# Compressed scores spread between the rows of two gate chunks, and three smaller moves around them

## The chip, the cores and the metric

The program runs on one core of a Trainium2 chip. A core has a matrix engine (TensorE, PE in the profile, with its weight loads as PEld), a vector engine (VectorE, DVE), a scalar engine (ScalarE, ACT), GpSimd (POOL), and queues that start DMA transfers (SP's queue here). Each engine works through its own list of instructions in the order in which the list was written; a semaphore holds an instruction back until what it needs is there. The metric is the time on the device of one execution, in microseconds, as the median of several runs.

## The reference

One layer of a decoder trunk on 256 tokens of 1024 channels, in float32:

```
h = rms_norm(x, norm_mix_g)
u_conv, q, kc, vc, ks, vs, kw, vw, g_heads, g_conv, g_attn = split(h @ w_in)
conv = silu(layer_norm(depthwise_31_taps(a * sigmoid(gate)))) @ conv_pw_w
o = g0 * attend(q, compressed kc, vc) + g1 * attend(q, ks, vs) + g2 * attend(q, kw, vw)
x = x + (sigmoid(g_conv) * conv + sigmoid(g_attn) * o) @ w_out
x = x + cross_attention(rms_norm(x, norm_x_g), mem, xq_w, xkv_w, xo_w)
x = x + swiglu(rms_norm(x, norm_ffn_g), ffn_in_w, ffn_out_w)
return rms_norm(x, final_norm_g)
```

There are 16 heads of 64 channels in 4 groups. With 256 tokens all four blocks of 64 keys are selected, so the selected and the window branch are two causal attentions over the same 256 positions with keys and values of their own; the compressed branch attends to 15 compressed blocks. `g0`, `g1`, `g2` are sigmoids of 48 logits per token (three for each head).

## The kernel before

**Products.** Each weight matrix is cut into chunks of 256 output channels, and each chunk comes by DMA in two halves of 128 x 1024 floats. A half is split into a high part (ScalarE copies it to fp32r, L173) and a low part (VectorE subtracts, L174; both in `split`). A chunk's product is six *rows* of eight matmuls with 256 columns each (`rows`, L238): for each half high times high, high times low, low times high. PE needs the high part for the first row of a half and the low part for its third. Raw halves have three buffers, high and low parts four each, so a transfer or a split starts when an earlier half has been used.

**Order.** The order of each engine's list is settled when the program is built, by a scheduler that goes by priorities; `in_line()` and `behind(...)` add orderings by hand (the first keeps a matmul behind the last row on PE, the second keeps what stands in it behind given instructions). The code order around the change is: convolution input (`u`), compressed keys and values (`kc`, `vc`), queries (`q0` to `q3`), then `ks`, `kw`, `vs`, `vw`, the 48 gate logits (`wg`, `g_ps`, L217 to L219, whose sigmoid `sgn` is L594 on ScalarE), the attention gates `ga0` to `ga3` (`gate(j)`), and the attention over eight pairs of heads, between whose parts the rows of `gc0` to `gc3` and `v0` to `v3` are dealt out by `rest(n)`.

**The convolution's taps** run beside all this. VectorE accumulates taps in PSUM (`taps_v`, L404, tiles `yp`), ScalarE multiplies taps (`taps_g`, L418, tiles `vw`, four buffers) for GpSimd to add (L420, `yt`); a few products are GpSimd's own (L416). `convolve(n_v, n_g, *marks)` issues the next `n_v` of VectorE's instructions and `n_g` of the other chain, behind its marks. `part67`, the last result of VectorE's taps, is added by GpSimd at L424. Note that `vw` in the profile is two things: the tap products (L416, L418, L420) and the weight chunk `vw` with its parts `vw_0h`, `vw_0l`, `vw_1h`, `vw_1l` (L173, L174, L238).

**Compressed scores.** After `ga0`, 32 matmuls of 32 columns (L650, `cs_ps`) give the scores of 16 heads in two halves of the queries. VectorE adds them to the bias (`nsc`, L653), takes the minimum, subtracts it (L655, L656) and spreads the compressed values over heads (L661, `vals`). Two transposes bring the sigmoids of the 48 gate logits to the layout of the queries (`gt_ps`, L669, after `ga1`), and VectorE takes the reciprocals (L670, L671).

**Attention.** For each pair of heads `scores` issues eight matmuls (L690, tile `s`, and L692, tile `s0`); VectorE adds the bias and takes the minimum (L695, L700), ScalarE exponentiates (L709, L713), VectorE normalizes (L716 to L723). One pass of the loop issues the scores of the next pair, some rows, the transposes of this pair's weights (`turned`: two of tile `pt_a`, then after one row `pt_b`, L734), whose copies ScalarE makes (`ptt_a`, `ptt_b`, L737), some rows more, and the weighted sums (`output`, tile `o`, L744 to L752). In the first pass the compressed weights are transposed too (`pc_ps`, L821; copy `pct`, L823).

**PSUM.** Tiles with one tag share buffers: "s0" has one (in turn `g_ps`, one half of the compressed scores, the gate transposes `gt_ps`, then the scores `s0` and `pt_b` of each pair), "o" has one, "s" and "pt" two each. A new tile waits until the last reader of the old one is done.

Of the kernel before, what the change touches and what calls it, by code (L numbers as in the profile page):

```python
# [15 lines left out]
P = 128  # L16
# [80 lines left out]
def tile_hybrid_block(  # L97
# [46 lines left out]
    def aux(name, shape, tag, bufs):  # L144
        return axp.tile(shape, F32, tag=tag, name=name, bufs=bufs)

    def f(ap):
        return ap.bitcast(F32)
# [20 lines left out]
    def split(w, shape, name):  # L169
        hi = small(f"{name}h", shape, F32R, tag="whi", bufs=4)  # L170
        lo = small(f"{name}l", shape, F32R, tag="wlo", bufs=4)
        with behind(*first.get(name, ())):
            nc.scalar.activation(hi, w, AF.Copy)  # L173
            nc.vector.tensor_tensor(out=lo, in0=w, in1=f(hi[:]), op=ALU.subtract)  # L174
        return hi, lo


    first = {}

    def behind(*marks):  # L180

# [42 lines left out]
    def in_line():  # L224
        return behind(*last)
# [321 lines left out]
    for j in range(4):  # L547
        ps = whole(f"q{j}", hf)
        q0, q1 = ([qt[j // 2][:, 4 * (j % 2) + 2 * b + k] for b in range(2)] for k in range(2))
        for b in range(2):  # L550
            nc.scalar.activation(q0[b][0:64], ps[0:64, b], AF.Copy, scale=-0.125)
            act = nc.scalar.activation(q1[b][64:128], ps[64:128, b], AF.Copy, scale=-0.125)
        for b in range(2):
            nc.vector.scalar_tensor_tensor(out=q0[b][64:128], in0=ps[0:64, b], scalar=-0.125, in1=f(q0[b][0:64]),
                                           op0=ALU.mult, op1=ALU.subtract)
            vec = nc.vector.scalar_tensor_tensor(out=q1[b][0:64], in0=ps[64:128, b], scalar=-0.125, in1=f(q1[b][64:128]),
                                                 op0=ALU.mult, op1=ALU.subtract)
        convolve((12, 11, 8, 3)[j], 5, act, vec)
        with behind(*last):
            if j == 0:  # L560
                hidden()
            elif j == 2:
                compressed()
# [16 lines left out]
    for br, name in enumerate(("vs", "vw")):  # L580
        ps = gemm_nat(name, h)
        act = nc.scalar.activation(vst[:, :, br], ps, AF.Copy)
        convolve(3, 3 + TAPS * br, act)
    ng = 3 * HEADS
    wg = small("wg", [P, NB, ng], tag="w", bufs=3)
    nc.sync.dma_start(wg, wgn)
# [43 lines left out]
            js = slice(j, j + 2)  # L630
            nc.vector.tensor_tensor(out=yt[:, js], in0=yt[:, js], in1=rl.unsqueeze(1).to_broadcast([P, 2, S]), op=ALU.mult)

    def gate(j):
        return nc.scalar.activation(sga[:, 2 * j:2 * j + 2], gemm(f"ga{j}", h), AF.Sigmoid)

    gate(0)


    sums = small("sums", [P, HEADS, 2, 2])
# [3 lines left out]
    def qh(hd, qb):  # L643
        return qt[hd // 8][:, hd % 8, qb * P:qb * P + P]

    for qb in range(2):
        cs_ps = aux(f"cs_ps{qb}", [P, HEADS, 2, 16], *(("s0", 1), ("s", 2))[qb])
        for hd in range(HEADS):
            with in_line():
                mm = nc.tensor.matmul(cs_ps[:, hd], lhsT=qh(hd, qb), rhs=kcp[:, hd // 4], start=True, stop=True)  # L650
        last[:] = [mm]
        for i in range(2):
            nc.vector.tensor_tensor(out=nsc[:, qb], in0=cs_ps[:, :, i], in1=nsc[:, qb], op=ALU.add)  # L653
    mc = small("mc", [P, 2, HEADS])
    nc.vector.tensor_reduce(out=mc, in_=nsc, axis=AX.X, op=ALU.min)  # L655
    vec = nc.vector.tensor_tensor(out=nsc, in0=nsc, in1=mc.unsqueeze(3).to_broadcast([P, 2, HEADS, 16]),  # L656
# [2 lines left out]
    with behind(vec):  # L659
        for i in range(2):  # L660
            nc.vector.tensor_tensor(out=vcm[:, 8 * i:8 * i + 8], in0=vcs[:, i].unsqueeze(1).to_broadcast([P, 8, HD]),  # L661
                                    in1=hm, op=ALU.mult)


    gate(1)
    four[0] = ""
    gt_ps = aux("gt_ps", [P, 2, ng], "s0", 1)
    for tb in range(2):
        nc.tensor.transpose(gt_ps[:, tb], sgn[:ng, tb * P:tb * P + P], ident[:ng, :ng])  # L669
    nc.vector.reciprocal(igc, gt_ps[:, :, 0:HEADS])  # L670
    nc.vector.reciprocal(igd.rearrange("p h t b -> p t b h"),  # L671
                         gt_ps[:, :, HEADS:3 * HEADS].rearrange("p t (b h) -> p t b h", b=2))
    gate(2)


    def heads_of(hp):
# [120 lines left out]
    for hp, n in enumerate((6, 6, 6, 5, 5, 5, 5, 4)):  # L797
        if hp < 7:
            p.append(scores(hp + 1))
            exp = weights(hp + 1, *p[hp + 1])  # L800

        with behind(*last):
            if hp == 2:
                total = layer_norm_squares(total)
            elif hp == 3:
                total = rnorm(total, "l")
            elif hp == 4:
                layer_norm_scale(total)
        m = max(n - 2, 2)
        rest(m)  # L810
        p0, p1 = p[hp]
        ta = [turned(f"a{hd}", [q for br in range(2) for q in (p0[:, k, br], p1[k][:, br, 0:P])])
              for k, hd in enumerate(heads_of(hp))]
        rest(1)
        tb = turned(f"b{hp}", [p1[k][:, br, P:S] for k in range(2) for br in range(2)])
        if hp == 0:
            pc_ps = aux("pc_ps", [P, 4, P], "pt", 2)
            with in_line():
                for qb in range(2):
                    for i in range(2):  # L820
                        mm = nc.tensor.transpose(pc_ps[:, 2 * i + qb], nsc[:, qb, 8 * i:8 * i + 8].rearrange("p h n -> p (h n)"), ident)  # L821
            last[:] = [mm]
            nc.scalar.activation(pct.rearrange("p i q -> p (i q)"), pc_ps.rearrange("p i q -> p (i q)"), AF.Copy)  # L823
        rest(n - m - 1)
        output(hp, ta, tb)


# [277 lines left out]
```

## Time and profile before

| what | value |
|---|---|
| median of 3 runs | 578.68 us (578.59 to 580.26) |
| the profiled execution's own time | 577.8 us |
| its span, first to last instruction | 576.0 us |
| mean granted TensorE clock | 0.993 |
| busy in the span | PE 559.3, PEld 512.3, DVE 428.3, ACT 364.1, POOL 148.5 us |
| moved by DMA | 97.22 MB, mean 169 GB/s |

The span is the profiled execution as the hardware profiler saw it; the execution's own time lies 1.8 us above it, and the median of the runs 0.9 us above that. "Busy" counts an engine's instructions from start to end; matmuls overlap, so a busy PE is not one that runs as fast as it could. The granted clock is the share of full speed that TensorE was given: 1.00 is 2.4 GHz, 0.50 is 1.2 GHz. The stage that the change touches runs from about 120 us (`ks`) to about 280 us (the first `pw` chunk). A row of the waits reads: engine, tile and line, what it waited for, microseconds in total, how many times, the longest. A row of the timeline reads: start, length, engine, line, operation, output and inputs with sizes, count, and in brackets the idle time before it with what ended it.

### The profile page before, as it was taken

The numbers are of one execution on the slowest core, as the hardware profiler recorded it, in microseconds if no ns is written. First come the engines' busy times: TensorE is split into PE (matmuls) and PEld (weight loads), VectorE is DVE, ScalarE is ACT, GpSimd is POOL, SyncE is SP. The second block draws the span as 40 slices with busy tenths as digits, with TensorE's granted clock in tenths as the row PEclk, the third lists the DMA queues.
The fourth block names the chain that finished last, engine by engine and source line by source line (L and its number), as shares of the span: only waits on it lengthen the run. The fifth ranks groups of instructions, "written<-read, shape, count | busy, mean of one in ns | idle before, by whom it ended". The sixth has DMA issues, their size and how long they took to land.

```text
span 576.0 us, 10272 instructions
## 1 busy us (share of the span) xinstructions
PE 559.3 (97%) x3892; PEld 512.3 (89%) x3892; DVE 428.3 (74%) x772; ACT 364.1 (63%) x687; POOL 148.5 (26%) x132
## 2 busy tenths in 40 slices
PE   9999999998998999989999999999999999999995
PEld 8999998898998878879999999998888888888884
DVE  3879999999678869886667775497877787865541
ACT  4768648689653966859746665376665566645431
POOL 0007997899993003300002200050000000000000
PEclk9999999999988999999999999999999999999999
DMA  8848814454454543422466642454655655766631
GB/s 308 336 140 259 308 34 144 135 174 147 149 181 149 151 155 98 134 87 77 140 243 207 206 150 77 147 173 147 203 174 158 217 181 176 213 184 206 195 116 73
DMA packets 29154, 97.22 MB, mean 169 GB/s; under 512 B 3120, under 2 KB 5552, under 8 KB 28848
## 3 DMA queue, kind: packets, MB, share of 16 engines
q1 hardware_dynamic: 28384, 95.25, 50.7%
q10 hardware_dynamic: 720, 1.31, 0.6%
q8 instruction: 30, 0.49, 0.3%
q14 instruction: 20, 0.16, 0.1%
HBM read 95.30 MB, written 1.25 MB: 168 GB/s over the span
## 4 chain that ended last, share of the span: by engine, by line
PE 81%; ACT 7%; POOL 5%; DVE 4%; issue 2%; DMA 1%; POOLq 0%; ACTq 0%; DVEq 0%
PE ps_f L950 14%; PE ps_u L238 8%; PE ps_f L952 7%; POOL yt L420 5%; PE ps_q L268 4%; PE ps_xq L238 4%; PE ps_pw L238 4%; PE ps_xo L238 4%; PE ps_wo L238 4%; PE fo L978 4%; PE fo L979 4%; PE fo L977 4%; PE ps_k L238 3%; PE ps_v L238 2%; PE ps_gc L238 2%
## 5 line engine op out<-in xcount | busy, mean ns | idle before, releaser
L420 POOL TENSOR_TENSOR yt<-yt,vw 128x512 f32<-128x512 f32 x65 | 99.8, 1536 | 53.7 <-DMA u<-in_wst_dram 46.1
L418 ACT ACTIVATE vw<-vt,ppt 128x256 f32<-128x256 f32 x110 | 47.8, 498 | 12.4 <-POOL yt L420 12.2
L404 DVE SCALAR_TENSOR_TENSOR yp<-vt,ppt,yp 128x256 f32<-128x256 f32 x100 | 48.5, 486 | 2.7
L950 PE MATMUL ps_f<-g,f_1h 128*128 128x512 f32 x176 | 48.8, 396 | 0.0
L994 POOL TENSOR_SCALAR x<-x,rr 128x512 f32<-128x512 f32 x1 | 0.7, 692 | 182.8 <-PE fo L979 182.8
L950 PE MATMUL ps_f<-g,f_0h 128*128 128x512 f32 x176 | 47.8, 397 | 0.0
L950 PEld LDWEIGHTS ps_f<-g,f_1h 128*128 128x128 f32 x176 | 32.6, 188 | 7.3
L174 DVE TENSOR_TENSOR f_0l<-f,f_0h 128x1024 fp32r<-128x1024 f32 x22 | 26.9, 1224 | 13.2 <-ACT f_0h L173 7.5
L950 PEld LDWEIGHTS ps_f<-g,f_0h 128*128 128x128 f32 x176 | 30.4, 188 | 4.6
L173 ACT ACTIVATE f_1h<-f 128x1024 fp32r<-128x1024 f32 x22 | 23.2, 1054 | 13.6 <-DMA f<-in_wst_dram 11.3
L174 DVE TENSOR_TENSOR f_1l<-f,f_1h 128x1024 fp32r<-128x1024 f32 x22 | 27.4, 1245 | 5.3 <-ACT f_1h L173 5.3
L952 PEld LDWEIGHTS ps_f<-g,f_0l 128*128 128x128 f32 x176 | 27.0, 189 | 3.9
L268 PE MATMUL ps_q<-hf,q 128*128 128x256 f32 x128 | 28.5, 381 | 0.0
L952 PE MATMUL ps_f<-g,f_1l 128*128 128x256 f32 x176 | 28.1, 281 | 0.0
L173 ACT ACTIVATE f_0h<-f 128x1024 fp32r<-128x1024 f32 x22 | 23.3, 1058 | 7.5 <-PE ps_f L950 4.1
L952 PE MATMUL ps_f<-g,f_0l 128*128 128x256 f32 x176 | 28.0, 281 | 0.0
L709 ACT ACTIVATE p<-p,mins 128x256 f32<-128x256 f32 x32 | 15.9, 498 | 18.0 <-DVE mins L695 18.0
L268 PEld LDWEIGHTS ps_q<-hf,q 128*128 128x128 f32 x128 | 24.1, 190 | 3.3
L953 ACT ACTIVATE ab<-ps_f 128x256 f32<-128x256 f32 x44 | 16.4, 373 | 12.5 <-PE ps_f L952 12.2
L952 PEld LDWEIGHTS ps_f<-g,f_1l 128*128 128x128 f32 x176 | 24.1, 189 | 0.0
L874 POOL COPY acc<-s_wo 128x256 f32<-128x256 f32 x1 | 0.7, 657 | 72.9 <-ACT s_wo L867 72.9
L954 DVE TENSOR_TENSOR ab<-ps_f,ab 128x256 f32<-128x256 f32 x44 | 18.0, 417 | 1.3 <-ACT ab L953 1.3
(542 smaller groups left out, 1605.8 us busy)
## 6 DMA issues: line engine op xcount, KB each, us to landing
f<-in_wst_dram SPq DMA_DIRECT2D x44, 512.0 KB, 4.9
fo<-in_wfo_dram SPq DMA_DIRECT2D x22, 512.0 KB, 4.6
u<-in_wst_dram SPq DMA_DIRECT2D x14, 512.0 KB, 6.2
q<-in_wst_dram SPq DMA_DIRECT2D x8, 512.0 KB, 5.7
ga<-in_wst_dram SPq DMA_DIRECT2D x8, 512.0 KB, 3.9
gc<-in_wst_dram SPq DMA_DIRECT2D x8, 512.0 KB, 3.7
v<-in_wst_dram SPq DMA_DIRECT2D x8, 512.0 KB, 3.8
pw<-in_wst_dram SPq DMA_DIRECT2D x8, 512.0 KB, 3.8
```

The lines of the kernel that those rows point to most:

```text
L173: nc.scalar.activation(hi, w, AF.Copy)
L174: nc.vector.tensor_tensor(out=lo, in0=w, in1=f(hi[:]), op=ALU.subtract)
L238: mm = nc.tensor.matmul(ps[:, b], lhsT=lhsT, rhs=rhs, start=row + b + kb == 0, stop=kb == NB - 1 and row == 2 and b == 1)
L268: mm = nc.tensor.matmul(ps[:, b], lhsT=w[:, k, cs], rhs=x[:, kb], start=kb + b == 0, stop=kb == NB - 1 and b == 1)
L404: nc.vector.scalar_tensor_tensor(out=out[:, i] if t == ts[-1] else acc[:, i], in0=v, scalar=w, in1=acc[:, i], op0=ALU.mult, op1=ALU.add)
L418: nc.scalar.activation(pr[:, i], v, AF.Identity, scale=w, bias=col(PP_DB, j + i) if t == 0 else 0.0)
L420: nc.gpsimd.tensor_tensor(out=y, in0=y, in1=pr, op=ALU.add)
L950: nc.tensor.matmul(ps, lhsT=hs[kb // 4][0][:, kb % 4, cs], rhs=fg[:, :, kb], start=kb == 0, stop=False)
L952: nc.tensor.matmul(ps[:, 1], lhsT=hs[kb // 4][1][:, kb % 4, cs], rhs=fg[:, 0, kb], start=False, stop=kb == NB - 1)
L977: nc.tensor.matmul(accs[c][tb], lhsT=th, rhs=hi[:, k], start=False, stop=False)
L978: nc.tensor.matmul(accs[c][tb], lhsT=th, rhs=lo[:, k], start=False, stop=False)
L979: nc.tensor.matmul(accs[c][tb], lhsT=tl, rhs=hi[:, k], start=False, stop=kb == NF - 1)
```

## The change

Four things are moved; no product is added or left out.

1. The 32 matmuls of the compressed scores become a generator, and `gate` takes three of them after each of its rows while there are any: 18 stand between the rows of `ga1`, 14 between those of `ga2`. Their PSUM tiles take the tag "pt". What VectorE does with them follows in the code after `ga2` (before: after `ga0`).
2. The gates' two transposes and the reciprocals stand behind `ga0` (before: behind `ga1`), and their tile `gt_ps` takes the tag "o" (before "s0", which the first pair's `s0` uses next).
3. VectorE's last nine tap instructions (three with `q3`, three with `vs`, three with `vw`) are all issued with `vw`, behind the low part of its second half (`vw_1l`).
4. In the attention loop the transposes `pt_a` come a row earlier and the sums two rows (before: one) after `pt_b`; in the first pass `pc_ps` stands ahead of `pt_a` with tag "o" (before behind `pt_b` with tag "pt").

```diff
-            nc.scalar.activation(hi, w, AF.Copy)
-            nc.vector.tensor_tensor(out=lo, in0=w, in1=f(hi[:]), op=ALU.subtract)
+            copy = nc.scalar.activation(hi, w, AF.Copy)
+            splits[name] = copy, nc.vector.tensor_tensor(out=lo, in0=w, in1=f(hi[:]), op=ALU.subtract)
...
-        convolve((12, 11, 8, 3)[j], 5, act, vec)
+        convolve((12, 11, 8, 0)[j], 5, act, vec)
...
-        convolve(3, 3 + TAPS * br, act)
+        convolve(2 * TAPS * br, 3 + TAPS * br, act, splits[name + "_1"][1])
...
-    def gate(j):
-        return nc.scalar.activation(sga[:, 2 * j:2 * j + 2], gemm(f"ga{j}", h), AF.Sigmoid)
+    def gate(j, few=iter(())):
+
+        ps = bank(f"ps_ga{j}")
+        for i in range(2):
+            for _ in rows(ps, halved(f"ga{j}", i), h, i):
+                for _ in range(3):
+                    next(few, None)
+        return nc.scalar.activation(sga[:, 2 * j:2 * j + 2], ps, AF.Sigmoid)
 
     gate(0)
+    gt_ps = aux("gt_ps", [P, 2, ng], "o", 1)
+    for tb in range(2):
+        nc.tensor.transpose(gt_ps[:, tb], sgn[:ng, tb * P:tb * P + P], ident[:ng, :ng])
+    nc.vector.reciprocal(igc, gt_ps[:, :, 0:HEADS])
+    nc.vector.reciprocal(igd.rearrange("p h t b -> p t b h"),
+                         gt_ps[:, :, HEADS:3 * HEADS].rearrange("p t (b h) -> p t b h", b=2))
...
-    for qb in range(2):
-        cs_ps = aux(f"cs_ps{qb}", [P, HEADS, 2, 16], *(("s0", 1), ("s", 2))[qb])
-        for hd in range(HEADS):
-            with in_line():
-                mm = nc.tensor.matmul(cs_ps[:, hd], lhsT=qh(hd, qb), rhs=kcp[:, hd // 4], start=True, stop=True)
-        last[:] = [mm]
-        for i in range(2):
-            nc.vector.tensor_tensor(out=nsc[:, qb], in0=cs_ps[:, :, i], in1=nsc[:, qb], op=ALU.add)
+    def compressed_scores():
+
+        for qb in range(2):
+            cs_ps = aux(f"cs_ps{qb}", [P, HEADS, 2, 16], "pt", 2)
+            for hd in range(HEADS):
+                with in_line():
+                    last[:] = [nc.tensor.matmul(cs_ps[:, hd], lhsT=qh(hd, qb), rhs=kcp[:, hd // 4], start=True, stop=True)]
+                yield
+            for i in range(2):
+                nc.vector.tensor_tensor(out=nsc[:, qb], in0=cs_ps[:, :, i], in1=nsc[:, qb], op=ALU.add)
+
+    few = compressed_scores()
+    gate(1, few)
+    four[0] = ""
+    gate(2, few)
+    for _ in few:
+        pass
...
-    gate(1)
-    four[0] = ""
-    gt_ps = aux("gt_ps", [P, 2, ng], "s0", 1)
-    for tb in range(2):
-        nc.tensor.transpose(gt_ps[:, tb], sgn[:ng, tb * P:tb * P + P], ident[:ng, :ng])
-    nc.vector.reciprocal(igc, gt_ps[:, :, 0:HEADS])
-    nc.vector.reciprocal(igd.rearrange("p h t b -> p t b h"),
-                         gt_ps[:, :, HEADS:3 * HEADS].rearrange("p t (b h) -> p t b h", b=2))
-    gate(2)
...
-        m = max(n - 2, 2)
-        rest(m)
-        p0, p1 = p[hp]
-        ta = [turned(f"a{hd}", [q for br in range(2) for q in (p0[:, k, br], p1[k][:, br, 0:P])])
-              for k, hd in enumerate(heads_of(hp))]
-        rest(1)
-        tb = turned(f"b{hp}", [p1[k][:, br, P:S] for k in range(2) for br in range(2)])
+        rest(n - 3)
         if hp == 0:
-            pc_ps = aux("pc_ps", [P, 4, P], "pt", 2)
+            pc_ps = aux("pc_ps", [P, 4, P], "o", 1)
...
-        rest(n - m - 1)
+        p0, p1 = p[hp]
+        ta = [turned(f"a{hd}", [q for br in range(2) for q in (p0[:, k, br], p1[k][:, br, 0:P])])
+              for k, hd in enumerate(heads_of(hp))]
+        rest(1)
+        tb = turned(f"b{hp}", [p1[k][:, br, P:S] for k in range(2) for br in range(2)])
+        rest(2)
         output(hp, ta, tb)
```

How the lists come to stand shows at three places.

VectorE's list from the queries' last parts to the first gate chunk. `yp` and `part` are taps, rows of L174 low parts of weights, `kdl` low parts of the keys. Before:

```order
L404 SCALAR_TENSOR_TENSOR yp_1191<-vt_354,ppt,yp_1191 128x256
L174 TENSOR_TENSOR kw_0l<-kw_1515,kw_0h 128x1024
L404 SCALAR_TENSOR_TENSOR yp_1191<-vt_354,ppt,yp_1191 128x256 x2
L174 TENSOR_TENSOR kw_1l<-kw_1545,kw_1h 128x1024
L404 SCALAR_TENSOR_TENSOR yp_1191<-vt_354,ppt,yp_1191 128x256
L174 TENSOR_TENSOR vs_0l<-vs_1596,vs_0h 128x1024
L404 SCALAR_TENSOR_TENSOR yp_1191<-vt_354,ppt,yp_1191 128x256 x2
L575 TENSOR_TENSOR kdl<-ps_ks,kdh 64x2x256 x4
L404 SCALAR_TENSOR_TENSOR yp_1191<-vt_354,ppt,yp_1191 128x256
L174 TENSOR_TENSOR vs_1l<-vs_1626,vs_1h 128x1024
L404 SCALAR_TENSOR_TENSOR part_361<-vt_354,ppt,yp_1191 128x256 x2
L174 TENSOR_TENSOR vw_0l<-vw_1673,vw_0h 128x1024
```

Now:

```order
L174 TENSOR_TENSOR kw_0l<-kw_1512,kw_0h 128x1024
L174 TENSOR_TENSOR kw_1l<-kw_1542,kw_1h 128x1024
L174 TENSOR_TENSOR vs_0l<-vs_1593,vs_0h 128x1024
L575 TENSOR_TENSOR kdl<-ps_ks,kdh 64x2x256 x4
L174 TENSOR_TENSOR vs_1l<-vs_1623,vs_1h 128x1024
L174 TENSOR_TENSOR vw_0l<-vw_1667,vw_0h 128x1024
L575 TENSOR_TENSOR kdl<-ps_kw,kdh 64x2x256 x4
L174 TENSOR_TENSOR vw_1l<-vw_1697,vw_1h 128x1024
L404 SCALAR_TENSOR_TENSOR yp_1191<-vt_354,ppt,yp_1191 128x256
L174 TENSOR_TENSOR wgl<-wg,wgh 128x384
L404 SCALAR_TENSOR_TENSOR yp_1191<-vt_354,ppt,yp_1191 128x256 x3
L174 TENSOR_TENSOR ga_0l<-ga_0_1801,ga_0h 128x1024
```

Nine tap instructions left the stretch ahead of `vw_1l`; they stand behind it, among `wgl` and the first gate chunk's low parts.

PE's list from the end of `ga0` on. Before:

```order
L238 MATMUL ps_ga_1800<-hh,ga_1l 128x256 x8
L650 MATMUL cs_ps_1865<-kcp,qt 128x32 x16
L650 MATMUL cs_ps_1884<-kcp,qt 128x32 x16
L238 MATMUL ps_ga_1908<-hh,ga_0h 128x256 x8
L238 MATMUL ps_ga_1908<-hl,ga_0h 128x256 x8
L238 MATMUL ps_ga_1908<-hh,ga_0l 128x256 x8
L238 MATMUL ps_ga_1908<-hh,ga_1h 128x256 x8
L238 MATMUL ps_ga_1908<-hl,ga_1h 128x256 x8
L238 MATMUL ps_ga_1908<-hh,ga_1l 128x256 x8
L669 MATMUL gt_ps<-cpt,sgn 128x48 x2
```

Now:

```order
L238 MATMUL ps_ga_1800<-hh,ga_1l 128x256 x8
L645 MATMUL gt_ps<-cpt,sgn 128x48 x2
L238 MATMUL ps_ga_1870<-hh,ga_0h 128x256 x8
L664 MATMUL cs_ps_1885<-kcp,qt 128x32 x3
L238 MATMUL ps_ga_1870<-hl,ga_0h 128x256 x8
L664 MATMUL cs_ps_1885<-kcp,qt 128x32 x3
L238 MATMUL ps_ga_1870<-hh,ga_0l 128x256 x8
L664 MATMUL cs_ps_1885<-kcp,qt 128x32 x3
L238 MATMUL ps_ga_1870<-hh,ga_1h 128x256 x8
L664 MATMUL cs_ps_1885<-kcp,qt 128x32 x3
```

The block of 32 short matmuls is gone; they stand three by three behind rows of eight. The two transposes moved ahead of it all, behind `ga0`.

ScalarE's list around the copies of the sixth pair of heads (`p_6` are the last exponentials of the pair after it, `pw_0h` is a later weight's high part). Before:

```order
L713 ACTIVATE p_6_2948,sums<-p_6_2948,mins 128x128 x4
L737 ACTIVATE ptt_a_3025<-pt_a_3020 128x512
L737 ACTIVATE ptt_a_3032<-pt_a_3027 128x512
L173 ACTIVATE pw_0h<-pw_0_3294 128x1024
L737 ACTIVATE ptt_b_3047<-pt_b_3042 128x512
```

Now:

```order
L723 ACTIVATE p_6_2948,sums<-p_6_2948,mins 128x128 x2
L747 ACTIVATE ptt_a_3010<-pt_a_3005 128x512
L723 ACTIVATE p_6_2948,sums<-p_6_2948,mins 128x128 x2
L747 ACTIVATE ptt_a_3017<-pt_a_3012 128x512
L747 ACTIVATE ptt_b_3039<-pt_b_3034 128x512
L173 ACTIVATE pw_0h<-pw_0_3294 128x1024
```

The copy `ptt_b`, which the sums wait for, stands ahead of the weight's copy now.

More of the change, by code (lines that the diff above doesn't have):

```diff
@@ L172, in split @@
         with behind(*first.get(name, ())):
-            nc.scalar.activation(hi, w, AF.Copy)
-            nc.vector.tensor_tensor(out=lo, in0=w, in1=f(hi[:]), op=ALU.subtract)
+            copy = nc.scalar.activation(hi, w, AF.Copy)
+            splits[name] = copy, nc.vector.tensor_tensor(out=lo, in0=w, in1=f(hi[:]), op=ALU.subtract)
         return hi, lo
-    first = {}
+    first, splits = {}, {}
     def behind(*marks):
```

## The prediction

> **What bounds the kernel now.** First the page's busy times and slices, then PE's waits.
>
> ```profile
> PE 559.3 (97%) x3892; PEld 512.3 (89%) x3892; DVE 428.3 (74%) x772; ACT 364.1 (63%) x687; POOL 148.5 (26%) x132
> PEclk9999999999988999999999999999999999999999
> ```
>
> PE is busy 97% of the span, so only three things can be gained: the 17 us in which it stands, the slices with a granted clock below full (here the two with an 8), and matmuls themselves, of which the change removes none.
>
> ```profile
> PE o L749 <- ACT ptt_b L737: 2.6, 3, 1.5
> PE s L692 <- DVE igd L671: 1.9, 1, 1.9
> PE ps_vs L238 <- DVE vs_1l L174: 1.5, 1, 1.5
> ...
> ```
>
> These are the longest; three more of its groups of waits (`pc_ps`, `vw`, `pct`) are shown where they count. All lie in the stage that is edited, as do both falls of the clock. The modelled end of a matmul hides part of a gap, so from here I count from start to start in PE's timeline; a row of eight without a wait takes 0.95 us (153.27 to 154.21 below).
>
> **Nine taps.** The timeline of PE, and of DVE below it:
>
> ```profile
> 139.11 1.09 PE L238 MATMUL ps_vs<-vs_1h,hl 128*128 128x256 f32 x8
> 141.72 1.21 PE L238 MATMUL ps_vs<-vs_1l,hh 128*128 128x256 f32 x8 [1.52 <-DVE vs_1l L174]
> 147.60 0.28 PE L218 MATMUL g_ps<-hl,wgh 128*48 128x256 f32 x1
> 148.71 1.20 PE L238 MATMUL ps_vw<-vw_1l,hh 128*128 128x256 f32 x8 [0.83 <-DVE vw_1l L174]
> 153.27 1.11 PE L238 MATMUL ps_ga<-hl,ga_0h 128*128 128x256 f32 x8
> 154.21 1.11 PE L238 MATMUL ps_ga<-hh,ga_0l 128*128 128x256 f32 x8
> 155.38 1.22 PE L238 MATMUL ps_ga<-hh,ga_1h 128*128 128x256 f32 x8
> ...
> 131.35 1.01 DVE L404 SCALAR_TENSOR_TENSOR yp<-vt,ppt,yp 128x256 f32<-128x256 f32 x2
> 139.96 1.71 DVE L174 TENSOR_TENSOR vs_1l<-vs,vs_1h 128x1024 fp32r<-128x1024 f32 x1
> 146.65 2.01 DVE L174 TENSOR_TENSOR vw_1l<-vw,vw_1h 128x1024 fp32r<-128x1024 f32 x1
> ```
>
> PE lost 141.72 − 139.11 − 0.95 = 1.66 us on `vs_1l`, 148.71 − 147.60 − 0.12 (one g_ps matmul) = 0.99 on `vw_1l`, and 1.17 − 0.95 = 0.22 on `ga_1h`. Seven of the nine taps stood ahead of `vs_1l`. At 0.5 us each (two in 1.01) they take 3.5 us, so VectorE could begin it at 139.96 − 3.5 = 136.5. The four key parts (`kdl`) and the high part ahead of it hold it back to about 137.5 by my count of the new list; it ends at 139.2, and PE asks at 139.11 + 0.95 = 140.06: no wait. `vw_1l` loses nine taps ahead of it and would end at 148.66 − 4.5 = 144.2, or at 145.5 where its own high part (ScalarE, not moved by the taps) sets the start; PE, 1.66 us earlier and without the two `g_ps` matmuls that filled in before, asks at 145.7. That margin is thin. I take all 2.87 us as gained; if `vw_1l` keeps its wait, 1.9. The nine taps behind `vw_1l`, 4.5 us, cost PE nothing while they fit the pauses in which VectorE stands for ScalarE, 4.9 us before `ga_1l` and 3.1 before a `ga_0l` (rows of the next fence). Without that cover the low parts of `ga0` would come up to 4.5 us later and PE with them. GpSimd, which waits for their result `part67` at L424, has seven more additions before it in the new list.
>
> **Transposes behind `ga0`: a new wait.** They need `sgn`, which ScalarE computes behind tap products that wait for GpSimd to free a buffer. GpSimd, ScalarE, PE and VectorE in turn:
>
> ```profile
> 147.67 3.14 POOL L416 TENSOR_SCALAR vw<-vt,ppt 128x256 f32<-128x256 f32 x2
> 152.10 0.91 ACT L418 ACTIVATE vw<-vt,ppt 128x256 f32<-128x256 f32 x2 [3.26 <-POOL yt L420]
> 157.78 0.36 ACT L594 ACTIVATE sgn<-g_ps 48x256 f32<-48x256 f32 x1
> 158.36 3.79 PE L650 MATMUL cs_ps<-kcp,qt 128*128 128x32 f32 x32
> 155.36 1.89 DVE L174 TENSOR_TENSOR ga_1l<-ga,ga_1h 128x1024 fp32r<-128x1024 f32 x1 [4.90 <-ACT ga_1h L173]
> 164.76 1.33 DVE L174 TENSOR_TENSOR ga_0l<-ga,ga_0h 128x1024 fp32r<-128x1024 f32 x1 [3.06 <-ACT ga_0h L173]
> ```
>
> PE, which left `ga0` at 158.36, now leaves it 2.87 us earlier, at 155.5. `sgn` ended at 158.14. If ScalarE's tap products came no earlier, PE would wait 2.6 us, with all of `ga1` and the bursts queued behind the transposes. But they do: the first of them waited until 152.10 for GpSimd, and there L424 (1.3 us, one addition) leaves the place ahead of it. The two L416, 3.14 us beside the split `vw_1l`, now run beside taps; earlier, beside `kdl`, two of them took 0.9 us, so that is up to 2.2 more. So `sgn` comes 1.3 to 3.5 us earlier, at 154.6 to 156.8, and the wait is 0 to 1.3 us. I take 0.5, nearer to the early end, because the split is over by then. The transposes themselves cost their 0.25 us as before.
>
> **Compressed scores and the clock.** PE again, and three windows, in each of which the number after POOL's is the granted clock:
>
> ```profile
> 161.99 2.05 PE L238 MATMUL ps_ga<-hh,ga_0h 128*128 128x256 f32 x8
> 165.36 1.11 PE L238 MATMUL ps_ga<-hh,ga_0l 128*128 128x256 f32 x8
> ...
> 158.30:161.90 3.60, 3.60 (x34) 3.60 (x33) 2.57 (x2) 1.86 (x3) 3.44 (x3) 0.97 0.73 218
> 161.90:165.00 3.10, 3.10 (x16) 3.10 (x16) 0.23 (x1) 2.12 (x4) 3.10 (x4) 0.50 0.64 211
> 184.00:260.00 76.00, 71.60 (x580) 64.53 (x580) 63.14 (x221) 56.95 (x161) 9.89 (x20) 1.00 0.41 129
> ```
>
> The 32 short matmuls took 161.99 − 158.36 = 3.63 us, 113 ns each. At their end the clock fell to 0.50 (from 2.4 to 1.2 GHz; until then PE had been busy without a gap), and the next two rows took 3.37 instead of 1.89 us: 1.48 lost. Spread out, each burst of three costs 0.34 us, 3.63 in all as before. That the clock holds I infer from the last row: from 184 to 260 us, where transposes and sums stand between rows and PE stands 4.4 us in all, it is 1.00 throughout. No row shows exactly this mix. I count 1.48 gained, with 0.3 off for the 11 changes of shape (a row after two short `mu` matmuls lost 0.1).
>
> The Trainium skill ("TensorE: Matmul & The Clock Gate", section "Back-to-back issue gap") gives a matmul of up to 64 columns about 60 cycles, 25 ns at the upper clock, when it stands alone. By that the 32 would take 0.8 us once weight loads hide behind long matmuls, and the sum would be 2.8 us lower; the trace's 113 ns speak against it.
>
> **The first pair's `s0`.**
>
> ```profile
> 175.50 0.40 PE L690 MATMUL s<-kdl,qt 128*128 128x512 f32 x1
> 177.75 0.35 PE L692 MATMUL s<-kdh,qt 128*128 128x256 f32 x1 [1.86 <-DVE igd L671]
> 178.76 1.89 PE L238 MATMUL ps_ga<-hh,ga_0h 128*128 128x256 f32 x8
> 182.15 1.12 PE L238 MATMUL ps_ga<-hh,ga_0l 128*128 128x256 f32 x8
> ...
> 174.62 2.30 DVE L174 TENSOR_TENSOR ga_0l<-ga,ga_0h 128x1024 fp32r<-128x1024 f32 x1
> 177.12 0.49 DVE L671 RECIPROCAL igd<-gt_ps 128x64 f32<-128x64 f32 x1
> ```
>
> `s0` waited for the reciprocal that reads its buffer, which was held up behind `ga_0l`. With tag "o" the last reader of "s0" is `sgn`, far earlier: 177.75 − 175.50 − 0.24 = 2.0 us gained. After this gap the clock fell again and two rows of `ga3` took 182.15 − 178.76 = 3.39 instead of 1.89 us: 1.5 gained, if PE has no gap like it here. What is late next would be `ga3`: its parts were split late, at 174.62, behind the scores' additions, the minimum and L661. In the new list both low parts stand ahead of all these, so I set nothing for it.
>
> **First pass and last copies.**
>
> ```profile
> 198.63 0.60 PE L734 MATMUL pt_b<-cpt,p 128*128 128x128 f32 x4
> 200.26 0.66 PE L821 MATMUL pc_ps<-cpt,nsc 128*128 128x128 f32 x4 [1.03 <-ACT ptt_a L737]
> 202.65 0.70 PE L744 MATMUL o<-pct,vals 128*128 128x256 f32 x2 [0.79 <-ACT pct L823]
> 254.95 0.59 PE L744 MATMUL o<-pct,vals 128*128 128x256 f32 x2
> 257.08 0.44 PE L749 MATMUL o<-ptt_b,vals 128*64 128x128 f32 x4 [1.54 <-ACT ptt_b L737]
> ...
> 186.35 0.58 ACT L634 ACTIVATE sga<-ps_ga 128x512 f32<-128x512 f32 x1
> 194.50 0.28 DVE L723 TENSOR_SCALAR p<-p,sums 128x128 f32<-128x128 f32 x1
> 255.50 1.05 ACT L173 ACTIVATE pw_0h<-pw 128x1024 fp32r<-128x1024 f32 x1
> ```
>
> First, whether the first pair is ready: its exponentials start behind the sigmoid of `ga3` (186.35) and its last weight is normalized at 194.78, 8.4 us later. PE has `gc0` (5.7 us), eight score matmuls (1.4), three rows (2.8) and `pc_ps` (0.4) before `pt_a`, 10.3: ready with 1.9 us to spare, into which L661 (3.5 us beside GpSimd, now between the minima and these) may bite.
>
> In the first pass PE lost 200.26 − 198.63 − 0.36 = 1.3 us before `pc_ps` and 202.65 − 200.26 − 1.36 = 1.0 before the sums. `pc_ps` in another buffer ends the first, and two rows cover the copies. But these come from ScalarE, busy with the next pair's exponentials, and in its list `ptt_b` ends some 0.9 us after PE asks. So 1.4 of 2.3 is gained. In later passes the count of rows between scores and sums does not change, and transposes a row earlier help only where ScalarE is free to copy. In the third pass it works without a pause and a weight's part still precedes the last copy; in the fourth the order of its copies is unchanged: no gain. In the sixth PE lost 257.08 − 254.95 − 0.53 = 1.6, and `pw_0h` (1.0 us of ScalarE) now follows `ptt_b`: 1.0 gained.
>
> **Sum**: 2.9 − 0.5 + 1.5 − 0.3 + 2.0 + 1.5 + 1.4 + 1.0 = 9.5 us. After 280 us nothing changes and PE sets the pace, so nothing is given back. The profiled execution's 577.8 becomes 568.3; the median lay 0.9 above it: **569.2 us**.
>
> **Rivals.**
> A, one term turns out empty: GpSimd's chain does not come earlier (2.6 instead of 0.5 us of wait, and a fall of the clock as after the gap at 175.7, 1.5), or the first pair's minima or exponentials come late behind `gc_1l` and L661, a stall of 2 to 4 us at `pt_a`. For it: both queues are in order and full there. Time 571.5 to 574.
> B, weight loads of short matmuls hide behind long ones: 11 of 32 hidden are 1.2 us, 568.0. By the Trainium skill's figure above it would be 566.4. Against it: in the window from 158.3 PEld is busy throughout (3.60 of 3.60), and it has a load for every long matmul too.
> C, slower: the bursts hold the clock at 0.50 through `ga1` and `ga2`. Each row at it costs 0.95 more, twelve 11.3, the short ones, if they double, 3.6: 580.5 to 584.1. It turns the sign from ten rows on (9.5 / 0.95). For it: the fall came just after short matmuls. Against: they are a quarter of the time here, and PE never stands.
> D, no change: everything gained is taken back by ScalarE, whose exponentials pace the passes: 578.7. Against: its waits there are for PE's scores and VectorE's minima, which move along.
>
> **How the numbers follow.** Forecast 0.61 (566.5 to 571.5), A 0.22, B 0.05, C 0.07, D 0.05. All gaps named, closed wholly, are 2.9 + 1.5 + 2.0 + 1.5 + 2.3 + 1.6 = 11.8 us, 566.9; B's 1.2 below it is 565.7, the low end. A's far end gives 574.5. Leaving C and D out, the range is 565.7 to 574.5. The measurement can tell about 0.3% (1.7 us) from no change; from the cases: faster 0.88, same 0.05, slower 0.07.
>
> **What would show it.** PE's waits without `vs_1l`, `vw_1l`, `igd` and `pc_ps`; one new wait of `gt_ps` for `sgn` under 1.3 us; a granted clock of 1.00 from 150 to 190; the first sums some 8 us earlier; `o` still waiting for `ptt_b`, about 2 us in all. A 0.50 among the bursts would prove C's mechanism, a wait of `pt_a` for VectorE A's. I am wrong if PE's gaps close and the end does not move.

## The result and the profile after

The changed kernel takes 569.71 us in the median of 4 runs (569.55 to 570.22), the kernel before 578.63 beside it (577.97 to 580.26): a ratio of 0.984, 95% interval 0.982 to 0.987, or 8.9 us. The forecast was 569.2. The profiled execution took 569.77 with a span of 568.0, so 8.0 us less than that of before; the changed kernel's median does not lie 0.9 above its profiled execution, as that of before did.

The page of the changed kernel, busy times and granted clock, then its waits of PE:

```profile
PE 555.8 (98%) x3892; PEld 509.8 (90%) x3892; DVE 429.8 (76%) x772; ACT 363.1 (64%) x687; POOL 149.9 (26%) x132
PEclk9999999999999999999999999999999999999999
```

```profile
PE o L759 <- ACT ptt_b L747: 2.1, 4, 0.8
PE ps_vw L238 <- DVE vw_1l L174: 1.4, 1, 1.4
...
PE pt_b L744 <- DVE mins L710: 0.5, 1, 0.5
PE ps_vs L238 <- DVE vs_1l L174: 0.2, 1, 0.2
```

The waits for `igd`, `pc_ps`'s copies and `pct` are gone, and so are both falls of the clock. Three things are not as forecast: `vw_1l` still holds PE up for 1.4 us, the new wait for `sgn` does not show in this list, and `pt_b` waits for VectorE's minima, which it did not do before.

PE's timeline (start, length, what) at the weight chunks `vs` and `vw`, and at the gates' transposes:

```profile
139.13 1.09 PE L238 MATMUL ps_vs<-vs_1h,hl 128*128 128x256 f32 x8
140.41 1.21 PE L238 MATMUL ps_vs<-vs_1l,hh 128*128 128x256 f32 x8 [0.18 <-DVE vs_1l L174]
145.18 1.09 PE L238 MATMUL ps_vw<-vw_1h,hl 128*128 128x256 f32 x8
147.63 1.20 PE L238 MATMUL ps_vw<-vw_1l,hh 128*128 128x256 f32 x8 [1.35 <-DVE vw_1l L174]
157.26 0.32 PE L645 MATMUL gt_ps<-cpt,sgn 48*128 48x48 f32 x2
```

From start to start, `vs_1l` costs 140.41 − 139.13 − 0.95 = 0.33 us (before 1.66) and `vw_1l` 147.63 − 145.18 − 0.95 = 1.50 (before 0.99). PE leaves `ga0` at 157.26 instead of 158.36, 1.1 us earlier where 2.9 were counted.

Now the view that decides this case and that the prediction did not read for this stage: the chain of waits, followed back from the end, in the kernel **before**, cut to the time from 160 to 205 us (start, length, what the end was waiting for at that time), and under it the first of the waits, from 140 to 200 us, of the queue that starts the loads:

```profile
160.70 2.15 POOL yt L420
...
169.50 0.70 DVE mc L655
...
171.22 1.61 DVE vals L661
...
172.92 1.78 DVE vals L661
174.70 2.24 DVE ga_0l L174
...
176.95 3.73 DMA gc<-in_wst_dram
...
180.79 1.06 ACT gc_1h L173
...
183.02 0.42 DVE p L695
...
202.12 0.49 ACT pct L823
...
202.65 0.70 PE o L744 x2
```

```profile
SPq L202 <- DVE ga_0l L174: 14.9, 4, 8.2
```

From 120.33 to 202.65 there is not one piece of PE in the chain. From 130 to 163 us it goes over GpSimd, mostly its additions (L420). From 166 us on the end waits for VectorE, which works through the minimum of the compressed scores, their subtraction and the two products `vals` (L661) before it comes to the low part of `ga3`; only when that is done is a weight buffer free, and the load of `gc` can start (the queue stood up to 8.2 us at a time for `ga_0l`); then come its high part, its low part, and behind it in VectorE's list the first pair's minima at 183.02, the exponentials, the copies, and at 202.65 PE's first weighted sums. PE's own gaps, both falls of the clock among them, lie *beside* this chain. (The chain is that of one execution, and PE's own work is nearly as long a path: several chains below go over PE.) The same view of the changed kernel:

```profile
160.78 2.27 POOL yt L420
...
164.47 0.95 ACT ga_1h L173
165.44 1.83 DVE ga_1l L174
167.29 4.50 DMA gc<-in_wst_dram
...
175.24 4.24 DMA gc<-in_wst_dram
...
195.27 0.59 ACT ptt_b L747
...
195.91 0.44 PE o L759 x4
```

PE is not in it here either up to 195.91, but `mc`, `vals` and the `ga_0l` behind them are gone from it. Three rows of VectorE's timeline in the changed kernel say why:

```profile
167.19 2.30 DVE L174 TENSOR_TENSOR ga_0l<-ga,ga_0h 128x1024 fp32r<-128x1024 f32 x1
...
177.38 0.67 DVE L676 TENSOR_REDUCE mc<-nsc 128x32 f32<-128x512 f32 x1
177.98 0.41 DVE L705 CUSTOM_DVE_ANT_0 p<-s,nb 128x256 f32<-128x256 f32 x1
```

Since the scores now come later, VectorE does the low parts of `ga3` first (`ga_0l` at 167.19 instead of 174.62); `mc` stands just ahead of the first pair's minima (L705), the subtraction and the products behind them, and the minima start at 177.98 instead of 183.02. From here on *the four instructions* are `mc`, the subtraction from `nsc`, and the two `vals`.

### The profile page after: what moved, and what is told of

It reads as the page before. It is cut to its first block, busy times and chain, and to the rows that moved or that the text cites. A ratio compares the mean times of both kernels' runs of the same rounds, so it can differ in the third digit from the quotient of the medians.

```text
span 568.0 us, 10270 instructions
## 1 busy us (share of the span) xinstructions
PE 555.8 (98%) x3892; PEld 509.8 (90%) x3892; DVE 429.8 (76%) x772; ACT 363.1 (64%) x687; POOL 149.9 (26%) x132
## 4 chain that ended last, share of the span: by engine, by line
PE 81%; ACT 9%; POOL 3%; DVE 2%; DMA 2%; issue 1%; POOLq 0%; ACTq 0%; DVEq 0%
PE ps_f L959 14%; PE ps_u L238 8%; PE ps_f L961 7%; PE ps_q L268 4%; PE ps_xq L238 4%; PE ps_pw L238 4%; PE ps_xo L238 4%; PE ps_wo L238 4%; PE fo L988 4%; PE fo L987 4%; PE fo L986 4%; POOL yt L420 3%; PE ps_k L238 3%; PE ps_v L238 2%; PE ps_gc L238 2%; DMA gc<-in_wst_dram 2%
## 5 line engine op out<-in xcount | busy, mean ns | idle before, releaser
L420 POOL TENSOR_TENSOR yt<-yt,vw 128x512 f32<-128x512 f32 x65 | 100.7, 1550 | 54.2 <-DMA u<-in_wst_dram 46.2
L174 DVE TENSOR_TENSOR f_0l<-f,f_0h 128x1024 fp32r<-128x1024 f32 x22 | 26.9, 1224 | 12.4 <-ACT f_0h L173 6.7
L174 DVE TENSOR_TENSOR f_1l<-f,f_1h 128x1024 fp32r<-128x1024 f32 x22 | 27.4, 1245 | 7.0 <-ACT f_1h L173 7.0
```

Of the source, the lines that this page charges most:

```text
L174: splits[name] = copy, nc.vector.tensor_tensor(out=lo, in0=w, in1=f(hi[:]), op=ALU.subtract)
L420: nc.gpsimd.tensor_tensor(out=y, in0=y, in1=pr, op=ALU.add)
```

## Experiments: the four parts, each alone

Each is the kernel before with one part of the change. The kernel before took 578.22 us beside them (20 runs).

**The spread scores** (part 1; transposes, taps and passes as before):

```diff
-    gate(1)
+    few = compressed_scores()
+    gate(1, few)
+    four[0] = ""
+    gt_ps = aux("gt_ps", [P, 2, ng], "s0", 1)
...
+    gate(2, few)
```

> The kernel before with one part of the change alone: the 32 compressed scores three by three behind the rows of ga1 and ga2, the transposes of the gates still in the buffer s0 and behind ga1, the nine taps and the first pass as before. Theory (the prediction's terms): the clock does not fall behind the short matmuls, 1.5 us gained; the changes of shape cost as good as nothing (the changed kernel showed 0.03 us for all 32). The wait of s0 for igd and the fall of the clock behind it stay, 2.0 and 1.5 us, since they belong to the transposes' buffer. So 1.5 us less than before, about 577.1 in the median, and the clock at 1.00 from 150 to 172 us. Rival: the two reciprocals now stand in VectorE's list behind the low parts of ga3 and the scores' additions, so that s0 waits longer; PE reaches it 1.5 us earlier and waits at least 1.5 us more, and the gain is zero or negative, 578.6 to 580.

573.01 us, ratio 0.991 (0.990 to 0.993): 5.2 less. Both theories were wrong. `s0` does not wait and the clock does not fall behind it, though the transposes have their old place and buffer. The chain of this kernel is PE's own work from 155.27 to 190.78.

**The transposes** (part 2):

```diff
     gate(0)
+    gt_ps = aux("gt_ps", [P, 2, ng], "o", 1)
```

> The kernel before with the gates' transposes and reciprocals alone moved behind ga0 and into the buffer o; the compressed scores stay one block of 32. Theory: s0 does not wait for igd (2.0 us) and the clock does not fall behind that gap (1.5), 3.5 us less, about 575.1; the fall behind the block of 32 stays, 0.50 at about 162 us. sgn is not earlier here, since the taps are not moved, but the transposes are asked for at the place where the block of scores began, so PE waits for sgn up to 0.3 us (it left ga0 at 158.36, sgn ended at 158.14). Rival: the clock falls behind s0's place for another reason (a change of shape at the first pair's scores), then only 2.0 us is gained, 576.6.

578.13 us in 10 runs, ratio 1.000 (0.999 to 1.001): nothing. And yet PE is, as expected, ahead: it starts `gc0` at 182.39 instead of 185.95, 3.6 us. Its waits in the first pass and its chain of waits say where they went:

```profile
PE pt_b L735 <- DVE mins L701: 2.1, 1, 2.1
...
PE pt_a L735 <- DVE p L724: 1.0, 1, 1.0
```

```profile
171.26 2.04 DVE vals L668 x2
...
174.66 2.31 DVE ga_0l L174
...
179.82 6.43 DMA gc<-in_wst_dram
186.35 1.06 ACT gc_1h L173
```

The chain over `vals` and `ga_0l` is where it was, and PE, being early, waits for it: 1.0 + 2.1, and 1.35 instead of 1.03 at `pc_ps`. Behind these new waits the clock is at 0.50 again, from 200.5 to 207.5 us. So the falls did not go away, they moved: the ten runs have a mean clock of 0.986 to 0.993, the kernel before mostly 0.991 to 0.994. (The profiled execution, 580.42, is the slowest of the ten.)

**The nine taps** (part 3):

```diff
-        convolve((12, 11, 8, 3)[j], 5, act, vec)
+        convolve((12, 11, 8, 0)[j], 5, act, vec)
...
-        convolve(3, 3 + TAPS * br, act)
+        convolve(2 * TAPS * br, 3 + TAPS * br, act, splits[name + "_1"][1])
```

> The kernel before with the nine taps alone moved behind vw_1l on VectorE. The prediction's term: 2.9 us less (vs_1l 1.66, vw_1l 0.99, ga_1h 0.22), 575.7. Theory after the changed kernel's trace: the splits that now run back to back, beside GpSimd's additions, get longer (kw_1l 1.41 to 2.3 us, vw_0l 1.53 to 2.3), vw_1l ends only 1.1 us earlier than before and PE leaves ga0 1.1 us earlier: 577.5, with a wait of 1.4 to 1.5 us of PE for vw_1l left. Rival: of these 1.1 us nothing reaches the end, because the first pair's s0 waits for the reciprocal as before: 578.6.

577.13 us, ratio 0.998 (0.997 to 0.999): 1.1 less, as the second theory said, with PE's wait for `vw_1l` at 1.4. PE leaves `ga0` at 157.50, 0.9 earlier.

**The passes** (part 4):

```diff
-        rest(m)
+        rest(n - 3)
...
-            pc_ps = aux("pc_ps", [P, 4, P], "pt", 2)
+            pc_ps = aux("pc_ps", [P, 4, P], "o", 1)
...
-        rest(n - m - 1)
+        rest(2)
```

> The kernel before with the passes' edit alone: two rows instead of one between the last transposes and the sums, and pc_ps in the buffer o. Theory: the first pass gains 1.0 us (2.3 us of waits, of which pt_b for VectorE's minima and the sums for ptt_b give back 1.3), the sixth 0.95, the seventh gives back 0.3 and the fourth 0.1: 1.6 us less than before, about 577.0. Rival: in the first pass the minima come late here for the same reason as in the changed kernel, and PE being 7 us later makes no difference, or the gain there is the 1.4 us of the prediction: 576.2.

575.75 us, ratio 0.996 (0.995 to 0.998): 2.5 less, near the prediction's 1.4 + 1.0 and more than expected here. Its profiled execution (576.59) shows something else: the clock never fell in it, neither behind the block of 32 nor behind the gap at `s0`. PE saved 3.0 us by that, and has three waits that are new or longer:

```profile
PE s L692 <- DVE igd L671: 2.3, 1, 2.3
...
PE pt_b L734 <- DVE mins L700: 1.9, 1, 1.9
...
PE gt_ps L669 <- DVE nsc L653: 1.0, 1, 1.0
```

The sum of the parts is 5.2 + 0.0 + 1.1 + 2.5 = 8.8 us, the whole 8.9.

## Experiments: VectorE's order

The new theory: the order that comes with the spread scores is what part 1 is worth. Three kernels move the four instructions and leave PE's list as it is. (The kernel before took 578.44 beside the first and third, 579.04 beside the second.)

**The transposes' part, and the four instructions behind the first pair's minima:**

```diff
+    with behind(*least):
+        mc = small("mc", [P, 2, HEADS])
+        nc.vector.tensor_reduce(out=mc, in_=nsc, axis=AX.X, op=ALU.min)
...
```

(`least` holds the last of the first pair's minima; the code stood ahead of `gate(1)`.)

> The kernel with the transposes' part alone (its time did not differ from before), and in it four instructions of VectorE moved and nothing else on any engine: the minimum of the compressed scores, their subtraction and the two products vals, which took 0.7 + 1.1 + 3.5 us ahead of the first low part of ga3, now stand behind the first pair's minima. New theory: the first pass was not held by PE's gaps alone but also by a second chain of nearly the same length (the low part of ga3, whose end frees a weight buffer, the load of gc, its high part on ScalarE, its low part on VectorE, then the first pair's minima and exponentials). With the four instructions out of its way that chain is 4 to 5 us earlier, and the 3.5 us that PE gains at s0 and by the clock reach the end: 574.7, between 574.0 and 575.5. Rival: something else holds the first pass (the second pair's minima, the copies), then little or nothing is gained: 577 to 578.2.

574.36 us, ratio 0.994 (0.992 to 0.995): 3.8 less than with the transposes' part alone. In both kernels `s0` does not wait, so this is what the order is worth once that gap of PE is closed.

**The kernel before, and the same edit alone:**

> The kernel before, and in it the same four instructions of VectorE (the minimum of the compressed scores, their subtraction, the two products vals) behind the first pair's minima; no other instruction of any engine has another place: the block of 32, the transposes behind ga1 in the buffer s0, the taps and the passes are as before. New theory: this order is what the spread scores brought (573.0 with the spread alone); the reciprocal igd comes 4 to 5 us earlier too, so that s0 does not wait: 574.4, as with the transposes' part and this order together, between 573.5 and 575. Rival: without the transposes' own part s0 still waits for igd behind the low part of ga3, 576 to 577.5.

574.11 us, ratio 0.991 (0.988 to 0.994): 4.9 less than the kernel before beside it, whose seven runs go from 577.63 to 580.87, and 4.1 less than the 578.22 of the 20 runs above. That is most of part 1 but not all: the spread scores alone took 573.01, 1.1 less than this. Block, place and buffer of the transposes are those of before; `igd` ends at 172.1 instead of 177.6, and `s0` does not wait. It also shows that with this order the transposes' part adds nothing (574.36 with it). Now the chain of waits is PE's own work:

```profile
162.67 8.38 PE ps_ga L238 x48
...
171.30 5.86 PE ps_ga L238 x48
...
178.56 5.68 PE ps_ga L238 x48
```

The first of these rows is 8.38 long instead of 5.68, because the clock fell behind the block and stayed down for over 6 us. This execution, 575.96, is the slowest of the four; the others took 574.01 to 574.17.

**The changed kernel, with the order of before put back:**

```diff
+            with behind(*late.get(name, ())):
+                splits[name] = copy, nc.vector.tensor_tensor(out=lo, in0=w, in1=f(hi[:]), op=ALU.subtract)
...
+    late["ga3_0"] = [vec]
```

> The changed kernel, with the first low part of ga3 on VectorE held behind those four instructions, as they stood before; TensorE's order stays as changed, so none of the gaps that the prediction counted comes back. The prediction's terms, which set nothing for this order: 569.7, no change. New theory: the chain over the weight buffer is late again by the 4 to 5 us by which the first pair's minima had come earlier (183.0 before, 178.0 in the changed kernel), less about 1 us of slack before the first transposes: 573.5, between 572.5 and 575.

(The loads and splits of `gc` come later with it, as they wait for the buffers.) 576.80 us, ratio 0.998 (0.997 to 0.999): 7.1 of the 8.9 us are lost, although PE's list has all that the change gave it. That is more than expected, and more than the old order costs: the scores are late here, so that `ga_0l` starts at 176.76, 2.1 later than in the kernel before. PE, being early, waits for this low part itself, after which the clock falls for two rows (1.5 us), and later for minima:

```profile
PE ps_ga L239 <- DVE ga_0l L175: 2.4, 1, 2.4
...
PE pt_b L746 <- DVE mins L712: 1.8, 1, 1.8
```

## Experiments: the block, the transposes and the splits

**The changed kernel with the 32 scores in one block, VectorE's order kept:**

```diff
-                for _ in range(3):
+                for _ in range(32):
...
+    with behind(*least):
```

> The changed kernel with the 32 compressed scores in one block behind the first row of ga1 instead of three by three, and VectorE's minimum, subtraction and products vals kept behind the first pair's minima as in the changed kernel (only the four additions of the scores come earlier). So the spreading alone is undone and VectorE's order kept. By the prediction's term the clock falls to 0.50 behind the block and costs 1.5 us: 571.2; if it stays down twice as long, as in the kernel with the nine taps alone, 572.7. Rival: the fall does not come, or the slack of the first pass covers it: 569.7 to 570.2.

570.35 us, ratio 0.986 (0.985 to 0.988), 0.6 above the changed kernel. The clock did not fall behind the block, as PE's timeline shows:

```profile
158.83 3.64 PE L664 MATMUL cs_ps<-kcp,qt 128*128 128x32 f32 x32
162.32 1.19 PE L238 MATMUL ps_ga<-hl,ga_0h 128*128 128x256 f32 x8
```

So without a fall of the clock spreading them is worth about 0.6 us by itself. What a fall would cost here this run does not show, since none came in its profiled execution.

**The changed kernel without the transposes' part:**

```diff
     gate(1, few)
     four[0] = ""
+    gt_ps = aux("gt_ps", [P, 2, ng], "s0", 1)
```

> The changed kernel without the part on the gates' transposes: they stand behind ga1 again and in the buffer s0, so that the first pair's s0 waits for the reciprocal igd. By the prediction's terms that is 2.0 us of wait and 1.5 of a fall of the clock: 573.2. New theory: with the spread scores the reciprocals come ahead of the late work on VectorE anyway (in the kernel with the spread alone s0 did not wait), PE asks here about 1 us earlier, so 0 to 1 us of wait: 569.7 to 570.7.

569.59 us, ratio 0.985 (0.983 to 0.987), the changed kernel's. With this order the second part is worth nothing: `s0` waits 0.04 us.

**Why the taps gave less than counted.** The low parts on VectorE, in the kernel before and then in the changed kernel (start, length, what):

```profile
132.26 1.41 DVE L174 TENSOR_TENSOR kw_1l<-kw,kw_1h 128x1024 fp32r<-128x1024 f32 x1
...
142.38 1.53 DVE L174 TENSOR_TENSOR vw_0l<-vw,vw_0h 128x1024 fp32r<-128x1024 f32 x1
```

```profile
131.37 2.32 DVE L174 TENSOR_TENSOR kw_1l<-kw,kw_1h 128x1024 fp32r<-128x1024 f32 x1
...
140.28 2.31 DVE L174 TENSOR_TENSOR vw_0l<-vw,vw_0h 128x1024 fp32r<-128x1024 f32 x1
...
145.44 2.13 DVE L174 TENSOR_TENSOR vw_1l<-vw,vw_1h 128x1024 fp32r<-128x1024 f32 x1
```

The six splits of `kw`, `vs` and `vw` take 12.1 us together instead of 9.8, beside GpSimd's additions (L420). One kernel leaves eleven of those additions out, so that its output lacks eleven taps:

```diff
-            if t > 0:
+            if t > 0 and not (j == 4 and 10 <= t <= 20):
```

> The changed kernel without eleven of GpSimd's additions (taps 10 to 20 of channels 512 to 767 of the convolution are not added into its sum, so its output lacks them); it is those that run while VectorE splits kw, vs and vw. ScalarE's high parts stand earlier in its list here too, as they no longer share it with products that wait for GpSimd. Theory: two engines on the same memory slow each other; without the additions the five splits from kw_1l to vw_1l, 2.32, 2.32, 1.57, 2.31 and 2.13 us long, take 1.2 to 1.3 each, VectorE is through with vw_1l at least 2 us earlier than 149.7, and PE's wait for it, 1.4, is gone: 568.0 to 568.5 if the first pass lets it through, 569.7 if it does not. Rival: the splits are long for another reason (their input arrives late) and stay above 2 us.

569.07 us, ratio 0.983 (0.980 to 0.985). The same splits without the additions, and the first of its waits of PE in this stage:

```profile
131.97 1.22 DVE L174 TENSOR_TENSOR kw_1l<-kw,kw_1h 128x1024 fp32r<-128x1024 f32 x1
...
139.79 1.23 DVE L174 TENSOR_TENSOR vw_0l<-vw,vw_0h 128x1024 fp32r<-128x1024 f32 x1 [0.58 <-ACT vw_0h L173]
...
145.56 1.47 DVE L174 TENSOR_TENSOR vw_1l<-vw,vw_1h 128x1024 fp32r<-128x1024 f32 x1 [0.55 <-ACT vw_1h L173]
```

```profile
PE ps_kw L238 <- ACT kw_0h L173: 1.4, 1, 1.4
```

That GpSimd's additions make the splits long is shown; a tap, which reads one of its inputs from PSUM, takes 0.5 us in all three kernels. The Trainium skill ("SBUF — State Buffer", section "Who interferes with whom") says that a VectorE instruction with two inputs in SBUF and a GpSimd instruction that reads SBUF hold each other off, the later one until the earlier is done; by that a split has to wait out up to one addition, an estimate of 1.22 + 1.3 us at most, and the trace's 2.3 agrees. For the time the run says less: it is 0.6 below the changed kernel, between the two cases named. Without the buffers shared with GpSimd ScalarE's list has another order, PE waits 1.4 us for `kw_0h` instead of `vw_1l`, and reaches `ga0` only 0.2 us earlier. (The 149.7 of the expectation is a slip: `vw_1l` ends at 147.57 in the changed kernel, and at 147.03 here.)

**Two tries at more.** The key parts of `kw` behind `wg`, with the transposes behind `ga1` in the buffer "o":

```diff
-        convolve(0, 3, act, vec)
+        convolve(0, 3, act, *([lows()] if br == 0 else []))
...
+    with behind(splits["wg"][1]):
+        lows()
```

> The changed kernel, with the four key parts kdl of kw behind the split of wg instead of ahead of vs_1l and vw_0l on VectorE, and the gates' transposes behind ga1 in the buffer o (so that sgn is not asked for early). VectorE begins the last splits about 0.9 us earlier (four kdl of 0.2 to 0.3 us each): PE's wait for vw_1l, 1.4, falls to 0.5 or less. By PE's gaps alone 568.7. Theory of the second chain: the first pass has under 1 us to spare there (pt_b waits 0.5 for the second pair's minima already), so 0.3 to 0.9 of it arrives: 569.0. Rival: nothing arrives, 569.7.

569.75 us, ratio 0.984 (0.981 to 0.987): the changed kernel's time. PE's wait for `vw_1l` is gone (the four key parts took 2.79 us, not 0.9) and the first pair's scores start 0.95 us earlier, but nothing arrives, as the rival said. Its low part on VectorE, and where PE pays:

```profile
143.55 1.24 DVE L174 TENSOR_TENSOR vw_1l<-vw,vw_1h 128x1024 fp32r<-128x1024 f32 x1 [1.01 <-ACT vw_1h L173]
```

```profile
PE pt_b L749 <- DVE mins L715: 1.9, 1, 1.9
```

The wait for the second pair's minima was 0.5 in the changed kernel, and no fall followed it; here the clock falls behind it, at 194 us. And with the transposes of later passes early as well:

```diff
-        rest(n - 3)
+        rest(n - 3 if hp == 0 else 1)
...
-        rest(2)
+        rest(2 if hp == 0 else n - 2)
```

> The kernel with the key parts behind wg, and in the second to eighth pass the first transposes pt_a one row after the scores instead of two or three before the end, so that ScalarE has two more rows for the copies. PE's waits of o for ptt_b in the changed kernel were 0.5 in the first pass and 0.8, 0.6 and 0.2 in the fourth, sixth and seventh. Theory: the last three close, 1.6 us less than with the key parts alone, about 567.3. Rival: ScalarE's copies then stand ahead of the next pair's exponentials, which become late for the next pass in turn, and nothing is gained: 569, or it is lost: 570.

571.49 us, ratio 0.987 (0.984 to 0.990): 1.7 slower than with the key parts alone. `ptt_b` still holds the sums up (four times, 1.8 in all), and a copy `ptt_a` does so for 0.7 in the third pass. No complete version tried beats the changed kernel; the one without its second part equals it with less.

## Why the prediction was right, point by point

The total was right (569.2 for 569.7), and part of the reason was not. That it came out is in part luck: the edit that spreads the scores also moved VectorE's work out of the way, and to that the prediction gave no price.

- **What bounds the kernel.** The prediction opened with "PE is busy 97% of the span, so only three things can be gained: the 17 us in which it stands, the slices with a granted clock below full", and summed PE's gaps. That step failed. Between 120 and 203 us the chain of waits did not touch PE; PE was 97% busy and still had slack. A gap closed there is gained only if the other chain moves too. "I am wrong if PE's gaps close and the end does not move", the prediction says; the transposes' part alone showed just that.
- **Clock fall 1.5, `s0` 2.0, clock fall behind it 1.5** (5.0 us of the 9.5). The sizes were right, a condition was missing. Closing the second and third alone gave 0.0, and an execution of the kernel before at a mean clock of 0.998 was no faster. With VectorE's new order the terms arrive: the order alone, which closes the second and third (3.5 counted), gave 4.1 to 4.9, and the spread scores, which close all three (5.0 counted), gave 5.2; the chain of both is PE's own work there. The prediction had the condition in hand in a sentence on the new list, "both low parts stand ahead of all these, so I set nothing for it". No run has the new order with the gap at `s0` left open, since the order closes that gap too; what the order alone would give with the gap in place is therefore not shown. Its check on the first pass, "ready with 1.9 us to spare", let the sigmoid of `ga3`, and the exponentials with it, come as much earlier as PE does. With the transposes alone PE began `gc0` 3.6 us earlier and that sigmoid 1.0 later, at 187.32 behind `gc_1h`; in the changed kernel it began at 180.55, because the load of `gc` had come earlier. Rival A named the right place (minima behind `gc_1l` and L661), as a danger of the change instead of the state that the change ends.
- **Nine taps 2.9.** Mis-sized: PE leaves `ga0` 1.1 earlier in the changed kernel, and alone the part gave 1.1. "Though that margin is thin" was the warning; what the count lacked was that splits freed from taps run beside additions and take 2.3 instead of 1.4 us. The lower case named there (1.9) was still too high.
- **Wait for `sgn` 0.5.** 0.1, and by luck: ScalarE ended `sgn` at 157.0, later than the 154.6 to 156.8 argued. Had PE left `ga0` at 155.5, as counted, it would have waited about 1.5 for it; PE left 1.8 later than that.
- **Changes of shape 0.3.** 0.03: the twelve rows and 32 short matmuls of `ga1` and `ga2` take 172.51 − 157.51 = 15.0 us, of which the rows 11.34, so the short ones 3.66 against 3.63 in the block. Rival B (hidden weight loads) is out by the same number, and C too: the clock was 1.00 through all bursts.
- **First pass 1.4, sixth pass 1.0.** 1.0 and 0.95, less 0.4 for `ptt_b` in the fourth and seventh pass, which the prediction had set at nothing; alone 2.5 in the median.
- **From the sum to the median.** The profiled executions differ by 8.0 instead of 9.5 us; that the changed kernel's median lies at its profiled time, and not 0.9 above it, gave 0.9 of it back. Two errors that partly cancel. (A slip of the range: its upper end, 574.5, is called rival A's far end, which the rival itself puts at 574.)

## What to carry to other kernels

Before summing the gaps of the busiest engine, read the chain of waits of that very stage: where it does not pass through that engine, closing that engine's gaps alone can buy nothing but new waits. If a change reorders two engines, put back the order of one alone: here PE's gaps were worth what had been counted only once four instructions on VectorE had moved. And look at what frees a load's buffer, because the instruction that holds a buffer can be the one that sets the time four steps later.

## What the runs showed of the hardware that was not expected

- The clock's fall behind the block of 32 short matmuls is not certain. It fell to 0.50 in five of the seven profiled executions that have the block (before, transposes alone, taps alone, and the two with the four instructions moved in the kernel before), and not in two (the passes alone, the changed kernel with the block). Where it fell it stayed down for over 3 us in three and for over 6 in two. In the seven profiles with bursts of three it fell behind none of them. What decides between fall and no fall the runs do not show.
- Nor does a fall decide the time where another chain sets it: of 20 runs of the kernel before one had a mean clock of 0.998 instead of 0.991 to 0.994 and took 578.21 us, the middle of the others; of seven more, those at 0.997 and 0.996 took 579.04 and 579.99.
- A split of 128 x 1024 on VectorE takes 1.22 us alone and up to 2.32 beside GpSimd's additions, which take 1.3 alone and 2.15 beside it.
